# Two input projections of the second layer as seven block products each, instead of plain tiled matmuls

## The chip, the cores and the metric

The kernel runs on one core of one Trainium2 chip. The metric is the device time of one execution in microseconds (us). Three runs of the kernel before gave 672.19, 672.62 and 673.32 us; the median is 672.62 us.

## The reference, cut to what matters

The reference is a decoder trunk of two layers over 512 tokens with a width of 1024, all in float32. The first layer is an attention layer, the second a gated linear recurrence (HGRN2). Each layer ends with a normed residual and a gated embedding. What the change touches is the start of the second layer:

```python
u = rms_norm(h, norm_pre[1])            # (512, 1024)
proj = u @ w_in                         # (1024, 4096)
q, fl, inp, g = jnp.split(proj, 4, axis=-1)   # each (512, 1024)
...
y = (o * jax.nn.silu(gh))               # gh is g by heads; inp enters the recurrence as i
```

`inp` (called i below) and `g` are each a product of a 512x1024 matrix with a 1024x1024 matrix.

## The kernel before

Activations are kept transposed: `h[k]` is a tile of 128 features by 512 tokens, with k from 0 to 7. Every operand of a matmul is held as a pair of float32r tiles, high part and low part, and one product of float32 precision takes three matmuls (`three`, L138 to L142: high by high, low by high, high by low). Weights come from memory in tiles of 128x1024 (512 KB) into one of three slots `w_raw`; `load_w` and `split` (L272 to L274) then make the pair: ScalarE (ACT) writes `w_hi`, VectorE (DVE) writes `w_lo` as the difference. `w_hi` and `w_lo` have two slots each.

The end of the first layer is `layer_tail`. There `lin_c` makes four feature blocks of the gate at once and `lin_a` makes the blocks o = 4 to 7 one after the other, 24 matmuls each. Behind each block, `gated` (L387 to L391) updates `h[o]`, and `nxt` writes the pair `xg[o]` of `h[o]` times the gain (L281, L282) and adds the square of `h[o]` to `ss_acc` (L226, L230), from which the root mean square of the second layer's input is made.

Then i and g are made in four quarters q of 512 columns each by `lin_b_tok`: 4 weight tiles and 96 matmuls of 512 columns a quarter, with `xg` as the stationary and the weights as the moving operand. Quarters 0 and 1 are i (into tiles `it`, tag b3h), 2 and 3 are g (into `sg`, tag b3l). The factor per token `r1` is applied when ACT copies a bank out of PSUM (`evac_tok`, L733). `r1` comes from `st.rstd()`: four tiny products on TensorE (L236), one small DVE instruction (L239) and a power on GpSimd (L252); `spread` (L259, L263) makes it a full tile `rbc`. In the code `rstd` stands between quarter 0 and quarter 1, and `spread` behind the first weight tile of quarter 1. With `rbc`, DVE and ACT make the normed pair `u` (`scaled_norm`, L288 and `split`), which the recurrence uses. The first weight tile of the recurrence has a pair of its own, `w_f0`.

The order of the instructions on each engine is set at build time. A planner walks the program with estimated costs; on each engine it issues, of the instructions that are ready, the one that stands earliest in the program, unless `first()` lifts it. Inside `tc.manual_schedule(engines={PE})` the instructions of TensorE keep the order of the program. Each queue then runs strictly in its order. All weight loads are issued on SyncE's queue (SP).

Of the kernel before, what the change touches and what calls it, by code (L numbers as in the profile page):

```python
# [10 lines left out]
F32 = mybir.dt.float32  # L11
F32R = mybir.dt.float32r
# [8 lines left out]
P = 128  # L21
# [25 lines left out]
def tile_fox_hgrn2(  # L47
# [29 lines left out]
    def psB():  # L77
        return ps.tile([P, S], F32, name="psB", tag="B", bufs=6)
# [25 lines left out]
    def col(c):  # L104
        return vecs[:, c:c + 1]
# [11 lines left out]
    def load_w(ap, dst=None, raw=None, eng=ve):  # L117
        if raw is None:
            raw = fetch(ap)
        if dst is None:  # L120
            dst = (wp.tile([P, D], F32R, name="w_hi", tag="w_hi", bufs=2),
                   wp.tile([P, D], F32R, name="w_lo", tag="w_lo", bufs=2))
        hi, lo = dst
        if isinstance(hi, list):

            for i in range(2):
                split(hi[i], lo[i], raw[:, i * S:(i + 1) * S], eng)
        else:
            split(hi, lo, raw, eng)
        return hi, lo  # L130
# [57 lines left out]
    def lin_b_tok(chunks, src, half, ready=(), between=None, at=0):  # L188

        banks = [psA(), psA(), psB(), psB()] if half % 2 == 0 else [psB() for _ in range(4)]  # L190
        for kp in range(4):
            w = ready[kp] if kp < len(ready) else None
            if not isinstance(w, tuple):
                w = load_w(chunks[kp], raw=w)
            for j in range(2):
                k = 2 * kp + j
                f = slice(j * 512, (j + 1) * 512)
                for t in range(NT):
                    c = slice(t * P, (t + 1) * P)
# [55 lines left out]
    def spread(r, copy=True):  # L255

        rb = psB()
        for t in range(NT):
            pe.matmul(out=rb[:, t * P:(t + 1) * P], lhsT=r[:, t:t + 1].broadcast_to([P, P]), rhs=ident, start=True, stop=True)  # L259
        if not copy:  # L260
            return rb
        rs = tmp.tile([P, S], F32, name="rbc", tag="rbc", bufs=1)
        ac.copy(rs, rb)  # L263
        return rs

    def slots(tag, dt=F32R, ks=range(KT)):
        return [big.tile([P, S], dt, name=f"{tag}{k}", tag=f"{tag}{k}") for k in ks]
# [9 lines left out]
    def split_scaled(dst_hi, dst_lo, src, s):  # L277
        if isinstance(s, float):
            ins = ac.mul(dst_hi, src, s)
        else:  # L280
            ins = ac.activation(out=dst_hi, in_=src, func=AF.Copy, scale=s)  # L281
        ve.scalar_tensor_tensor(out=dst_lo, in0=src, scalar=s, in1=dst_hi.bitcast(F32), op0=ALU.mult, op1=ALU.subtract)  # L282
        return ins.ins

    def scaled_norm(dst, k, src, gcol, rb):

        un = t2("un")
        ve.scalar_tensor_tensor(out=un, in0=src, scalar=col(gcol + k), in1=rb, op0=ALU.mult, op1=ALU.mult)  # L288
        split(dst[0][k], dst[1][k], un)
# [46 lines left out]
            with first(o == KT - 1):  # L336
                ac.activation(out=self.zg[o], in_=b, func=AF.Copy, scale=col(C_NPOST[self.layer] + o))

    def layer_tail(layer, h, ah, zg, last=False):

        st = ah.st = Stat()
        ah.zg, hm = zg, ah.mem
        for g in ah.begun:
            for _ in g:
                pass
        for o in range(len(ah.begun), KT - 1):
            eng = gp if not last and o == len(ah.begun) else ve
# [16 lines left out]

        ws = [load_w(wgC[layer, c]) for c in range(2)]
        raws = [fetch(wgC[layer, c]) for c in range(2, 4)]

        def low(k):
            ve.tensor_tensor(out=hm[1][k], in0=h[k], in1=hm[0][k].bitcast(F32), op=ALU.subtract)

        with tc.manual_schedule(engines={DVE}):
            for k in range(KT):
                with first():
                    t = t2("zn")
                    ve.tensor_tensor(out=t, in0=rb, in1=zg[k], op=ALU.mult)
                    ve.tensor_tensor(out=h[k], in0=h[k], in1=t, op=ALU.add)
                    ac.copy(hm[0][k], h[k])
                    if k:
                        low(k - 1)
                if k in (4, 6):  # L380
                    ws.append(load_w(None, raw=raws[k // 2 - 2]))
            with first():
                low(KT - 1)
        for o, b in zip(LATE, eb):
            ac.copy(ah.ple(o), b)

        def gated(o, b, f=slice(0, S)):  # L387
            sg = t2("sgm")[:, f]
            ac.activation(out=sg, in_=b[:, f], func=AF.Sigmoid)  # L389
            ve.tensor_tensor(out=sg, in0=sg, in1=ah.ple(o)[:, f], op=ALU.mult)  # L390
            ve.tensor_tensor(out=h[o][:, f], in0=h[o][:, f], in1=sg, op=ALU.add)  # L391
            if last:
                nc.sync.dma_start(out[o][:, f], h[o][:, f])
            else:
                nxt(o)

        if not last:
            xg = pair_big("b2")
            stn = Stat()

            def nxt(o):
                split_scaled(xg[0][o], xg[1][o], h[o], col(C_NPRE[1] + o))
                stn.add(h[o])

        banks = lin_c(ws, hm)
        ws = [load_w(wgA[layer, o]) for o in range(2)]
        for o, b in enumerate(banks):
            gated(o, b)
        for o in range(4, KT):
            w = ws.pop(0)  # L410
            if last and o == KT - 1:
# [12 lines left out]
        return None if last else (xg, stn)
# [281 lines left out]
        nc.sync.dma_start(h[k], xT[:, k, :])  # L706
    att.close()
    turn[1] = 4
    xg, st = layer_tail(0, h, ah, slots("b3h", F32))

    l1 = ctx.enter_context(tc.tile_pool(name="l1", bufs=1))


    lmin = const.tile([P, 1], F32, name="lmin")
# [9 lines left out]
    it = slots("b3h", F32)  # L728
    sg = slots("b3l", F32)
    u = pair_big("b1")  # L730
    def evac_tok(q, banks):
        for t in range(NT):
            ac.activation(out=(it, sg)[q // 2][2 * t + q % 2], in_=banks[t], func=(AF.Copy, AF.Silu)[q // 2], scale=r1[:, t:t + 1])  # L733

    banks = lin_b_tok(wB1[0:4], xg, 0)
    r1 = st.rstd()
    rb = []
    banks1 = lin_b_tok(wB1[4:8], xg, 1, between=lambda: rb.append(spread(r1)))
    evac_tok(0, banks)
    for k in range(KT):  # L740
        scaled_norm(u, k, h[k], C_NPRE[1], rb[0])
    evac_tok(1, banks1)
    for q in range(2, 4):
        evac_tok(q, lin_b_tok(wB1[4 * q:4 * q + 4], xg, q))

    y = pair_big("b2")

# [1 line left out]
        pass  # L749


    w_f0 = load_w(wA1[8], [l1.tile([P, D], F32R, name=f"w_f0{q}") for q in range(2)])

    def general(rp):

# [299 lines left out]
    with tc.If(ok > 0) as cmp:  # L1055
        with tc.tile_pool(name="rec", bufs=2) as rp:
            ah = bounded(rp)
        layer_tail(1, h, ah, it, last=True)
    with cmp.Else():
        with tc.tile_pool(name="rec", bufs=2) as rp:  # L1060
            general(rp)
        ah = Ahead(1, y, ple_l1)
        ah.load(0)
        ah.room(u)
        ah.load1()
        for part in range(3):
            ah.load_emb(part)
        for o in EARLY:
            for _ in ah.early(o):
                pass  # L1070
        layer_tail(1, h, ah, it, last=True)


_INS = ["xT", "pT", "vec", "wfl", "wA0", "wB0", "wA1", "wB1", "wo", "wgC", "wgA", "wpl"]
# [61 lines left out]
```

## Time and profile before

| | |
|---|---|
| median of three runs | 672.62 us (672.19 to 673.32) |
| the profiled execution's own time | 672.09 us |
| its span in the profile | 670.3 us |
| TensorE busy in the span | 657.3 us, 98% |
| VectorE busy | 434.6 us, 65% |
| ScalarE busy | 336.9 us, 50% |
| GpSimd busy | 39.6 us, 6% |

The span runs from the first to the last instruction; the execution's own time is 1.8 us longer. TensorE's records overlap, since matmuls are pipelined, so its busy share is read as "had work", and its speed from the distance of starts. In the text, quarter 0 of i begins at 352.9 us of the span, and the recurrence's first matmul on `w_f0` at 441.9 us.

### The profile page before, as it was taken

Reading aid. Unit: us, or ns where it says so; the run is one execution under the profiler, and the core shown is the slowest. Engines: PE = TensorE matmul, PEld = TensorE weight load, DVE = VectorE, ACT = ScalarE, POOL = GpSimd, SP = SyncE. Lnnn points to the kernel's source line nnn. Section 1 sums busy time; section 2 is a strip of 40 time slices with the busy share of each in tenths; the row PEclk is TensorE's granted clock in tenths of the full one; section 3 lists DMA queues with packets and bytes.
Section 4 is the critical chain, followed back from the end, with each engine's and each line's share of the span. In section 5 each row is a group of like instructions: output and inputs, shape, how many; then the busy total and the mean of one; then the engine's idle time right before and its main releaser. Section 6 shows DMA issues by size and latency. Waiting matters only on the chain.

```text
span 670.3 us, 8922 instructions
## 1 busy us (share of the span) xinstructions
PE 657.3 (98%) x3226; PEld 548.4 (82%) x3226; DVE 434.6 (65%) x893; ACT 336.9 (50%) x656; POOL 39.6 (6%) x45
## 2 busy tenths in 40 slices
PE   8999999999999998999999999999999998999996
PEld 5888888888888877888888888888888887888886
DVE  7596223888888897337694372329888888233963
ACT  6457223766767685444563453344445455433431
POOL 1102200000000061001000110000010000001000
PEclk9999999999999999999999999999999999999999
DMA  7311326655555573221223223321122124122121
GB/s 283 130 64 65 128 95 189 165 151 133 153 139 139 150 230 100 95 95 37 92 92 125 84 79 109 135 68 64 63 70 89 63 93 135 56 96 95 58 107 59
DMA packets 26578, 73.22 MB, mean 109 GB/s; under 512 B 3808, under 2 KB 4192, under 8 KB 26528
## 3 DMA queue, kind: packets, MB, share of 16 engines
q1 hardware_dynamic: 26528, 72.59, 33.9%
q8 instruction: 27, 0.44, 0.3%
q14 instruction: 23, 0.19, 0.1%
HBM read 57.76 MB, written 2.10 MB: 89 GB/s over the span
## 4 chain that ended last, share of the span: by engine, by line
PE 92%; DVE 5%; ACT 1%; DMA 1%; issue 1%; POOL 0%; SPq 0%; ACTq 0%; DVEq 0%; POOLq 0%
PE psA L140 17%; PE psA L141 17%; PE psA L142 17%; PE psB L140 7%; PE psB L142 7%; PE psB L141 7%; PE psB L638 2%; PE psB L653 1%; PE psB L615 1%; PE psB L652 1%; PE psB L614 1%; PE psA L182 1%; PE psA L183 1%; PE psA L185 1%; PE psB L183 1%; PE psB L185 1%
## 5 line engine op out<-in xcount | busy, mean ns | idle before, releaser
L274 DVE TENSOR_TENSOR w_lo<-w_raw,w_hi 128x1024 fp32r<-128x1024 f32 x91 | 111.6, 1228 | 104.1 <-ACT w_hi L273 98.8
L140 PE MATMUL psA<-b1h,w_hi 128*128 128x512 f32 (+1 forms) x384 | 154.6, 403 | 0.0
L142 PE MATMUL psA<-b1l,w_hi 128*128 128x512 f32 (+1 forms) x384 | 148.5, 387 | 0.0
L141 PE MATMUL psA<-b1h,w_lo 128*128 128x512 f32 (+1 forms) x384 | 148.2, 386 | 0.2 <-DVE w_lo L274 0.2
L273 ACT CAST w_hi<-w_raw 128x1024 fp32r<-128x1024 f32 x92 | 96.2, 1047 | 62.4 <-PE psB L141 42.1
L142 PEld LDWEIGHTS psA<-b1l,w_hi 128*128 128x128 f32 x384 | 72.1, 188 | 15.1
L140 PEld LDWEIGHTS psA<-b1h,w_hi 128*128 128x128 f32 x384 | 72.3, 188 | 12.9 <-ACT sgm L389 0.7
L141 PEld LDWEIGHTS psA<-b1h,w_lo 128*128 128x128 f32 x384 | 72.5, 189 | 12.6 <-DVE w_lo L274 0.6
L140 PE MATMUL psB<-w_hi,b2h 128*128 128x512 f32 x144 | 56.3, 392 | 0.0
L142 PE MATMUL psB<-w_lo,b2h 128*128 128x512 f32 x144 | 56.1, 389 | 0.0
L141 PE MATMUL psB<-w_hi,b2l 128*128 128x512 f32 x144 | 56.1, 389 | 0.0
L621 ACT ACTIVATE pp<-pp,nm 128x128 f32<-128x128 f32 (+3 forms) x64 | 36.2, 565 | 23.0 <-DVE nm L619 22.2
L619 DVE CUSTOM_DVE_ANT_0 pp<-psB,cmask 128x128 f32<-128x128 f32 (+3 forms) x64 | 30.7, 480 | 14.5 <-PE psB L638 11.2
L230 DVE TENSOR_TENSOR ss_acc<-ss_acc,sq 128x512 f32<-128x512 f32 x26 | 17.9, 690 | 28.9 <-ACT sq L226 28.7
L140 PE MATMUL psA<-b2h,w_hi 128*128 128x512 f32 x80 | 31.8, 397 | 0.0
L142 PEld LDWEIGHTS psB<-w_lo,b2h 128*128 128x128 f32 x144 | 27.0, 188 | 5.7
L141 PEld LDWEIGHTS psB<-w_hi,b2l 128*128 128x128 f32 x144 | 27.1, 188 | 5.5
L140 PEld LDWEIGHTS psB<-w_hi,b2h 128*128 128x128 f32 x144 | 27.0, 188 | 5.5
L274 DVE TENSOR_TENSOR PTl<-psB,PTh 128x128 fp32r<-128x128 f32 (+3 forms) x64 | 30.8, 482 | 1.0 <-ACT PTh L273 0.8
L638 PE MATMUL psB<-ident,pp 128*128 128x128 f32 x160 | 28.4, 276 | 2.9 <-DVE pp L624 1.5
L142 PE MATMUL psA<-b2l,w_hi 128*128 128x512 f32 x80 | 31.2, 390 | 0.0
L141 PE MATMUL psA<-b2h,w_lo 128*128 128x512 f32 x80 | 31.2, 390 | 0.0
(228 smaller groups left out, 1217.5 us busy)
## 6 DMA issues: line engine op xcount, KB each, us to landing
w_raw<-in_wA_dram SPq DMA_DIRECT2D x40, 512.0 KB, 3.2
w_raw<-in_wB_dram SPq DMA_DIRECT2D x23, 512.0 KB, 3.3
w_raw<-in_wo_dram SPq DMA_DIRECT2D x16, 512.0 KB, 3.8
h<-in_xT_dram SPq DMA_DIRECT2D x16, 256.0 KB, 6.0
h<-kh SPq DMA_DIRECT2D x32, 128.0 KB, 2.3
w_raw<-in_wgC_dram SPq DMA_DIRECT2D x8, 512.0 KB, 3.2
w_raw<-in_wgA_dram SPq DMA_DIRECT2D x8, 512.0 KB, 3.3
h<-qh SPq DMA_DIRECT2D x16, 128.0 KB, 2.3
```

The source lines that it names most:

```text
L140: pe.matmul(out=out_ps, lhsT=sta[0], rhs=mov[0], start=start, stop=False)
L141: pe.matmul(out=out_ps, lhsT=sta[1], rhs=mov[0], start=False, stop=False)
L142: pe.matmul(out=out_ps, lhsT=sta[0], rhs=mov[1], start=False, stop=stop)
L182: pe.matmul(out=b, lhsT=hi[:, c], rhs=src[0][k], start=k == 0, stop=False)
L183: pe.matmul(out=b, lhsT=lo[:, c], rhs=src[0][k], start=False, stop=False)
L185: pe.matmul(out=b, lhsT=hi[:, c], rhs=src[1][k], start=False, stop=k == KT - 1)
L230: ve.tensor_tensor(out=self.acc, in0=self.acc, in1=sq, op=ALU.add)
L273: ins = ac.copy(dst_hi, src)
L274: eng.tensor_tensor(out=dst_lo, in0=src, in1=dst_hi.bitcast(F32), op=ALU.subtract)
L619: ve.tensor_tensor_reduce(out=pp[:, :W], in0=sc[:, :W], in1=cmask[:, S - W:S], op0=ALU.add, op1=ALU.min, scale=1.0, scalar=-NEG, accum_out=nm)
L621: ac.activation(out=pp[:, :W], in_=pp[:, :W], func=AF.Exp, bias=nm, scale=-1.0, accum_out=den)
L638: pe.transpose(out=tp[:, kt * P:(kt + 1) * P], in_=pp[:, kt * P:(kt + 1) * P], identity=ident)
```

## The change

The 512x1024 by 1024x1024 product is cut into two by two blocks: the activations by token halves (rows) and feature halves (columns), the weights by 512x512 blocks. Instead of eight block products, seven are made, of sums and differences of blocks, and the results are sums of these seven. Each block product (`product`) takes 24 matmuls of 512 columns, with two weight tiles, and uses two PSUM banks of tag B; i and g together take 14 products.

- The sums of activation blocks (`SM_D` to `SM_G`) are made in the tail of the first layer by `pair`, behind `nxt(o)` for o = 4 to 7: two multiplications on ACT, four subtractions or additions of 128x256 on DVE, and one `split` of 128x1024, into `a_sum`, a pool of its own. For o below 4, `xg` is made for the first 256 tokens alone.
- The sums of weight blocks are made in place. `t1` (two tiles, with `w_f0`'s slots) is loaded with B11 and split, and then B12 is added by an accumulating DMA that GpSimd's queue issues (`more`). `t2s` is `t1` plus B22, added on DVE; B12 is then accumulated onto the tile of B22, and B21 onto `t2s`. In each matrix six tiles are accumulated, six are loaded plainly and two are added on DVE.
- The order of the products is p1, p2, p3, p6, p7, p4, p5; p1 and p2 take plain blocks. For i, `rstd` and `spread` both stand between p1 and p2, on TensorE in that order.
- The results are collected in the tiles `it` and `sg`: ACT copies p1, DVE adds each further product out of PSUM in place, 14 additions of 128x512 a matrix, and ACT applies `r1` in place (with Silu for g).
- `scaled_norm` stands in the program between i and g.

```diff
             def nxt(o):
-                split_scaled(xg[0][o], xg[1][o], h[o], col(C_NPRE[1] + o))
+                f = slice(0, S // 2 if o < 4 else S)
+                split_scaled(xg[0][o][:, f], xg[1][o][:, f], h[o][:, f], col(C_NPRE[1] + o))
                 stn.add(h[o])
+                if o >= 4:
+                    pair(h, o - 4)
...
+    a_sum = [[sums.tile([P, 4, TH], F32R, name=f"as{q}{k}") for k in range(4)] for q in range(2)]
+    def tsum(q, c):
+        return (l1, sums)[q].tile([P, D], F32, name=f"tsum{q}{c}", tag=f"tsum{q}{c}")
+    def pair(h, k):
+        un = []
+        for b in (k, k + 4):
+            un.append(t2("un"))
+            ac.mul(un[-1], h[b], col(C_NPRE[1] + b))
+        a11, a21, a12, a22 = [x[:, i * TH:(i + 1) * TH] for x in un for i in range(2)]
+        sm = tsum(1, k % 2).rearrange("p (j t) -> p j t", t=TH)
+        ve.tensor_tensor(out=sm[:, SM_D, :], in0=a21, in1=a22, op=ALU.subtract)
+        ve.tensor_tensor(out=sm[:, SM_E, :], in0=sm[:, SM_D, :], in1=a11, op=ALU.subtract)
+        ve.tensor_tensor(out=sm[:, SM_F, :], in0=a11, in1=a21, op=ALU.subtract)
+        ve.tensor_tensor(out=sm[:, SM_G, :], in0=a12, in1=sm[:, SM_E, :], op=ALU.add)
+        split(a_sum[0][k], a_sum[1][k], sm)
...
+    def product(kind, ws):
+        banks = [psB(), psB()]
+        for k in range(4):
+            w, f = ws[k // 2], slice(k % 2 * S, (k % 2 + 1) * S)
+            hi, lo = operand(kind, k)
+            for t in range(2):
+                c = slice(t * P, (t + 1) * P)
+                three(banks[t], (hi[:, c], lo[:, c]), (w[0][:, f], w[1][:, f]), k == 0, k == 3)
+        return banks
+    def block(m, i, j, c):
+        return wB1[8 * m + 4 * j + 2 * i + c]
+    def more(dst, ap):
+        gp.dma_start(dst, ap, accum_op=ALU.add)
+        return dst
...
+        t1 = [tsum(0, c) for c in CH]
+        for c in CH:
+            nc.sync.dma_start(t1[c], block(m, 0, 0, c))
+        w = loads(t1)
+        for c in CH:
+            more(t1[c], block(m, 0, 1, c))
+        p1 = product((0, 0), w)
+        w = [load_w(block(m, 1, 0, c)) for c in CH]
+        if between:
+            between()
+        for t in CH:
+            ac.copy(C(1, 0, t), p1[t])
+        p2 = product((0, 1), w)
+        b22 = [fetch(block(m, 1, 1, c)) for c in CH]
+        w = loads(b22)
+        plus(0, 0, p2, (1, 0))
+        end(0, 0)
+        p3 = product(SM_G, w)
+        t2s = [tsum(1, c) for c in CH]
+        for c in CH:
+            ve.tensor_tensor(out=t2s[c], in0=t1[c], in1=b22[c], op=ALU.add)
+            more(b22[c], block(m, 0, 1, c))
+        w = loads(t2s)
+        p6 = product(SM_E, w)
+        for c in CH:
+            more(t2s[c], block(m, 1, 0, c))
+        w = loads(b22)
+        plus(1, 0, p6, (1, 0))
+        plus(0, 1, p3, (1, 0), ALU.subtract)
+        p7 = product(SM_F, w)
+        w = loads(t2s)
+        plus(1, 1, p7, (1, 0))
+        p4 = product((1, 1), w)
+        w = loads(t1)
+        plus(1, 0, p4, (1, 1))
+        end(1, 0)
+        p5 = product(SM_D, w)
+        for i in CH:
+            plus(i, 1, p5, (i, 1), (ALU.add, ALU.subtract)[i])
+            end(i, 1)
...
-    banks = lin_b_tok(wB1[0:4], xg, 0)
-    r1 = st.rstd()
...
-    for q in range(2, 4):
-        evac_tok(q, lin_b_tok(wB1[4 * q:4 * q + 4], xg, q))
+    def rstd1():
+        nonlocal r1
+        r1 = st.rstd()
+        rb.append(spread(r1))
+    with tc.manual_schedule(engines={PE}):
+        token_major(0, it, rstd1)
+        for k in range(KT):
+            scaled_norm(u, k, h[k], C_NPRE[1], rb[0])
+        token_major(1, sg)
+    att.close()
...
-    w_f0 = load_w(wA1[8], [l1.tile([P, D], F32R, name=f"w_f0{q}") for q in range(2)])
+    w_f0 = load_w(wA1[8], [l1.tile([P, D], F32R, name=f"w_f0{q}", tag=f"tsum0{q}") for q in range(2)])
```

## Rows read from the trace of the kernel before

**Rows 1.** The page, part 1: busy us (share of the span) and instructions.

```profile
PE 657.3 (98%) x3226; PEld 548.4 (82%) x3226; DVE 434.6 (65%) x893; ACT 336.9 (50%) x656; POOL 39.6 (6%) x45
```

**Rows 2.** Windows: stretch, length, then busy us by engine, clock, DMA share, GB/s.

```profile
331.10:357.60 26.50, 26.50 (x118) 21.79 (x118) 25.88 (x38) 18.05 (x28) 0.00 (x0) 1.00 0.24 83
...
352.89:441.90 89.01, 89.01 (x401) 73.80 (x400) 33.54 (x43) 34.29 (x44) 3.82 (x6) 1.00 0.29 101
```

**Rows 3.** Lines by form, TensorE, 352.80 to 441.92 us: busy, mean ns, idle.

```profile
L140 PE MATMUL psB<-w_hi,b2h 128*128 128x512 f32 x96 | 37.6, 391 | 0.0
...
L140 PE MATMUL psA<-w_hi,b2h 128*128 128x512 f32 x32 | 12.5, 391 | 0.0
```

**Rows 4.** Waits of TensorE, whole span: total us, times, longest; the longest first.

```profile
PE psA L140 <- ACT b2h L281: 1.6, 1, 1.6
```

**Rows 5.** Timeline of the statistic: start, duration, engine, line [idle before, releaser].

```profile
374.75 0.94 PE L236 MATMUL psB<-ones,ss_acc 128*128 128x1 f32 x8
375.55 0.49 PE L140 MATMUL psB<-w_hi,b2h 128*128 128x512 f32 x1
...
375.73 0.16 DVE L239 TENSOR_SCALAR ms<-psB 128x4 f32<-128x4 f32 x1 [4.14 <-PE psB L236]
...
375.97 1.93 POOL L252 TENSOR_TENSOR rs<-ms,mhalf 128x4 f32<-128x4 f32 x1 [71.13 <-DVE ms L239]
...
377.94 0.69 ACT L733 ACTIVATE b3h<-psA,rs 128x512 f32<-128x512 f32 x1 [2.17 <-POOL rs L252]
...
381.14 1.05 PE L259 MATMUL psB<-ident,rs 128*128 128x128 f32 x8
381.95 0.48 PE L140 MATMUL psB<-w_hi,b2h 128*128 128x512 f32 x1
```

**Rows 6.** Lines by form, VectorE, 331.1 to 357.6 us, the tail.

```profile
L274 DVE TENSOR_TENSOR w_lo<-w_raw,w_hi 128x1024 fp32r<-128x1024 f32 x5 | 6.1, 1219 | 0.0
L282 DVE SCALAR_TENSOR_TENSOR b2l<-h,vecs,b2h 128x512 fp32r<-128x512 f32 x8 | 6.0, 747 | 0.2 <-ACT b2h L281 0.2
```

**Rows 7.** Timeline of VectorE at the end of the tail.

```profile
354.45 0.69 DVE L391 TENSOR_TENSOR h<-h,sgm 128x512 f32<-128x512 f32 x1
355.06 1.22 DVE L274 TENSOR_TENSOR w_lo<-w_raw,w_hi 128x1024 fp32r<-128x1024 f32 x1
356.19 0.75 DVE L282 SCALAR_TENSOR_TENSOR b2l<-h,vecs,b2h 128x512 fp32r<-128x512 f32 x1
356.86 0.69 DVE L230 TENSOR_TENSOR ss_acc<-ss_acc,sq 128x512 f32<-128x512 f32 x1
```

**Rows 8.** Timeline of VectorE near the span's end: additions of 128x256.

```profile
665.71 0.43 DVE L390 TENSOR_TENSOR sgm<-sgm,b3l 128x256 f32<-128x256 f32 x1 [1.99 <-ACT sgm L389]
666.17 0.42 DVE L391 TENSOR_TENSOR h<-h,sgm 128x256 f32<-128x256 f32 x1
```

**Rows 9.** Timeline of one weight tile: its slot's release, both parts, the next tile.

```profile
363.84 1.05 ACT L273 CAST w_hi<-w_raw 128x1024 fp32r<-128x1024 f32 x1 [4.34 <-PE psB L141]
...
364.92 1.22 DVE L274 TENSOR_TENSOR w_lo<-w_raw,w_hi 128x1024 fp32r<-128x1024 f32 x1 [4.17 <-ACT w_hi L273]
...
363.86 0.39 PE L140 MATMUL psA<-w_hi,b2h 128*128 128x512 f32 x1
```

**Rows 10.** Timeline of VectorE: an addition out of PSUM and what follows.

```profile
306.39 0.69 DVE L375 TENSOR_TENSOR zn<-psB,b3h 128x512 f32<-128x512 f32 x1 [2.42 <-PE psB L259]
307.12 0.69 DVE L376 TENSOR_TENSOR h<-h,zn 128x512 f32<-128x512 f32 x1
```

**Rows 11.** Timeline of VectorE: the norms of `u` with a weight tile between.

```profile
387.12 2.07 DVE L288 SCALAR_TENSOR_TENSOR un<-h,vecs,rbc 128x512 f32<-128x512 f32 x3
389.11 1.22 DVE L274 TENSOR_TENSOR w_lo<-w_raw,w_hi 128x1024 fp32r<-128x1024 f32 x1
390.25 1.89 DVE L274 TENSOR_TENSOR b1l<-un,b1h 128x512 fp32r<-128x512 f32 x3
```

**Rows 12.** The page, part 6: DMA issues, KB each, median us to landing.

```profile
w_raw<-in_wB_dram SPq DMA_DIRECT2D x23, 512.0 KB, 3.3
```

More of the change, by code (lines that the diff above doesn't have):

```diff
@@ L337, in evac, with layer_tail @@
                 ac.activation(out=self.zg[o], in_=b, func=AF.Copy, scale=col(C_NPOST[self.layer] + o))
-    def layer_tail(layer, h, ah, zg, last=False):
+    def layer_tail(layer, h, ah, zg, pair=None):
+        last = pair is None
         st = ah.st = Stat()
@@ L708, in tile_fox_hgrn2 @@
     turn[1] = 4
-    xg, st = layer_tail(0, h, ah, slots("b3h", F32))
     l1 = ctx.enter_context(tc.tile_pool(name="l1", bufs=1))
+    sums = att.enter_context(tc.tile_pool(name="sums", bufs=1))
+    TH = S // 2
+    SM_D, SM_E, SM_F, SM_G = range(4)
+    a_sum = [[sums.tile([P, 4, TH], F32R, name=f"as{q}{k}") for k in range(4)] for q in range(2)]
[13 more added lines that the diff above has]
+        split(a_sum[0][k], a_sum[1][k], sm)
+    xg, st = layer_tail(0, h, ah, slots("b3h", F32), pair)
     lmin = const.tile([P, 1], F32, name="lmin")
@@ L730, in tile_fox_hgrn2, with operand @@
     u = pair_big("b1")
-    def evac_tok(q, banks):
-        for t in range(NT):
-            ac.activation(out=(it, sg)[q // 2][2 * t + q % 2], in_=banks[t], func=(AF.Copy, AF.Silu)[q // 2], scale=r1[:, t:t + 1])
-    banks = lin_b_tok(wB1[0:4], xg, 0)
-    r1 = st.rstd()
-    rb = []
[L738 to L742, printed above, removed]
-    for q in range(2, 4):
-        evac_tok(q, lin_b_tok(wB1[4 * q:4 * q + 4], xg, q))
+    def operand(kind, k):
+        if isinstance(kind, int):
+            return [a_sum[q][k][:, kind, :] for q in range(2)]
+        row, c = kind
+        return [xg[q][k + 4 * c][:, row * TH:(row + 1) * TH] for q in range(2)]
@@ new lines, in tile_fox_hgrn2, with token_major, C, plus @@
+    CH = range(2)
+    def token_major(m, dst, between=None):
+        def C(i, j, t):
+            return dst[2 * (2 * i + t) + j]
+        def plus(i, j, bank, src, op=ALU.add):
+            for t in CH:
+                ve.tensor_tensor(out=C(i, j, t), in0=bank[t], in1=C(*src, t), op=op)
+        def end(i, j):
+            for t in CH:
+                q = 2 * i + t
+                ac.activation(out=C(i, j, t), in_=C(i, j, t), func=AF.Silu if m else AF.Copy, scale=r1[:, q:q + 1])
+        def loads(raws):
+            return [load_w(None, raw=raw) for raw in raws]
+        t1 = [tsum(0, c) for c in CH]
[8 more added lines that the diff above has]
+            between()
+        for t in CH:
+            ac.copy(C(1, 0, t), p1[t])
[27 more added lines that the diff above has]
+            end(i, 1)
@@ L746, in tile_fox_hgrn2 @@
+    r1 = None
+    rb = []
+    def rstd1():
[8 more added lines that the diff above has]
+    att.close()
     y = pair_big("b2")
@@ L1057, in tile_fox_hgrn2 @@
             ah = bounded(rp)
-        layer_tail(1, h, ah, it, last=True)
+        layer_tail(1, h, ah, it)
     with cmp.Else():
@@ L1070, in tile_fox_hgrn2 @@
                 pass
-        layer_tail(1, h, ah, it, last=True)
+        layer_tail(1, h, ah, it)
 _INS = ["xT", "pT", "vec", "wfl", "wA0", "wB0", "wA1", "wB1", "wo", "wgC", "wgA", "wpl"]
```

## The prediction

> **What bounds the kernel now.** I read the page first. TensorE has work in 98% of the span, and no other engine comes near [rows 1]. A busy share alone could hide waits, so I looked at the list of TensorE's waits: the longest is 1.6 us, and it lies at the start of the kernel [rows 4]. Then I took the window that the change rebuilds, from the first matmul of i to the first of the recurrence: 89.01 us, TensorE busy throughout, its clock at 1.00 [rows 2], with 384 weight matmuls, 128 on each of three lines, of which the one is shown [rows 3]. The two breaks for the statistic cost 0.80 us (374.75 to 375.55) and 0.81 us (381.14 to 381.95) [rows 5]. So a matmul costs (89.01 - 1.61) / 384 = 0.2276 us, and 24 of them 5.46 us. This stage is bound by TensorE alone; VectorE works 33.5 of its 89 us [rows 2].
>
> The reader should look just as hard at the 26.5 us before and around its start. In the tail of the first layer VectorE is busy for 25.88 of 26.50 us [rows 2]. TensorE doesn't notice, because what VectorE finishes last, the sum of squares at 356.86 + 0.69 = 357.55 us [rows 7], isn't needed until 374.75 us [rows 5]. There are 17 us of cover there, and they are what the change spends.
>
> **The matmuls removed.** Fourteen products of 24 are 336 matmuls, 48 fewer: 48 x 0.2276 = -10.9 us. Shapes and operand types stay, so I take the same price.
>
> **The statistic, moved.** Now quarter 0 is followed by a mean, and the spread comes a weight tile later, so the way from the mean's end (375.55) over VectorE (375.73) and GpSimd (375.97 and 1.93 us) to the first reader (377.94) runs beside matmuls [rows 5]. After the change mean and spread follow each other on TensorE, with nothing between: 377.94 - 375.55 = 2.4 us in which TensorE stands still. This is sure, as its order is fixed. p2 and all behind it queue up there.
>
> And the mean comes after 24 matmuls, not after 96: if p1 starts at 352.9, it ends at 358.4, while the sum of squares was ready at 357.55 before any work was added to VectorE. What is added ahead of it: the planner takes the earliest ready instruction of the program, and `pair` for blocks 0 to 2 stands ahead of `gated(7)`. One `pair` is four operations of 128x256, 0.43 us each and 0.46 from start to start where one feeds the next [rows 8], and a low part of 128x1024, which takes 1.13 us of the queue (355.06 to 356.19) [rows 7]: 4 x 0.44 + 1.13 = 2.9 us, three of them 8.7 us. Half of `xg` for four blocks saves 4 x 0.26 = 1.0 us (0.69 for 128x512 less 0.43 for 128x256 [rows 8, 10]). The gaps that can be filled are 26.50 - 25.88 = 0.6 us. So the sum of squares ends at 357.55 + 8.7 - 1.0 - 0.6 = 364.6 us. Of the weight tiles' low parts in that window two belong to the new stage; if none of them gets ahead of it, it is 2.3 us earlier, 362.3; if the added work on ScalarE (per pair two multiplications and a cast, some 2.5 us) makes VectorE wait here and there, I allow 1 us more, 365.6. I take 364.6, as both weight tiles ran in that place before [rows 6, 7].
>
> Then p2 begins at 364.6 + 0.8 + 2.4 + 0.8 = 368.6. Without any wait it would begin at 352.9 + 5.5 + 1.6 = 360.0. Loss: +8.6 us (6.3 to 9.6). p1 itself may start up to six us late without changing this, since TensorE waits for the sum of squares anyway. p3 waits for the fourth pair (2.9 us) and four more weight tiles (4 x 1.13): 364.6 + 7.4 = 372.0, in time for 368.6 + 5.5 = 374.1. Loss there: nothing.
>
> **Weight tiles, twice as fast.** A tile now feeds 12 matmuls, not 24. Its successor's high part starts when its slot is free, at the start of the next tile (363.84 against 363.86), and the low part ends at 364.92 + 1.22 = 366.14, 2.30 us later [rows 9]. It is needed by the third matmul of the tile after: 2.73 + 0.46 = 3.19 us. Slack 0.9 us, where there were 3.6. An instruction on VectorE that starts just before it costs 0.6 (out of PSUM, 306.39 to 307.12 for one that feeds the next, 0.6 otherwise [rows 10]), 0.66 (norms, 387.12 to 389.11 for three [rows 11]) or 1.13 us (a weight sum). Most fit, two in a row don't.
>
> VectorE's sum for i, from p2's start to p5's end, six products or 32.8 us: 12 low parts at 1.13 (13.6), two weight sums (2.3), ten additions out of PSUM at 0.65 (6.5), the norms of `u` at (1.99 + 1.80) / 3 = 1.26 each (10.1; 1.80 is 1.89 less the overlap of 0.08 that the norms show, 2.07 against 1.99), and the fourth pair (2.9): 35.4 us. That is 2.6 us too much if the norms, which stand ahead of g in the program, all run there; if they spill into g there is room, as g needs 14 x 1.13 + 2.3 + 14 x 0.65 = 27.2 of 38.2 us. Between 0 and 2.6, I take 1.4. ScalarE has 14 casts of 1.05 us and 10 smaller pieces a matrix and stays well under 38 us.
>
> **The accumulating DMAs.** No row shows one. A plain load of 512 KB lands in 3.3 us [rows 12]. An accumulating one reads a second stream, so I bound it by 3.3 and 9.9 us. The tightest is B12 onto B22's first tile: issued when the weight sum is made, some 3.6 us into p3 (two additions out of PSUM, one low part, one sum), needed when p7's first high part may start, 2 x 5.46 - 2.73 = 8.2 us into p3, with the slack of 0.9: 5.5 us. At 3.3 it costs nothing, at 9.9 it costs 4.4 us in i, and in g less, where VectorE is free earlier. For a doubled transfer, 6.6 us, it is 1 us late. The reload of `t1` for g is about as tight (5.46 - 2.30 = 3.2 us against 3.3). I take 0.6 us for all of it, nearer to the plain row, since two other tiles are always in flight unhurried. On GpSimd's queue the accumulations onto `t1` stand ahead of the power of the statistic, but they wait only for p1's split, done before 364. The Trainium skill (DMA: Bandwidth & Descriptors, Anatomy of one DMA) gives 2.0 us plus bytes over 436 GB/s for a DMA issued by GpSimd, an estimate of 3.2 us here; by it the sum would be 0.6 us lower.
>
> What moves without a price: 16 evacuations on ScalarE become additions and scalings beside other products; SyncE's queue issues fewer loads; `w_f0` in `t1`'s slots can be split once p5's second tile is, a product ahead of its use; the recurrence's pool lies where the sums lay and must wait for p5, but its first tiles are wanted after 24 more matmuls.
>
> **Sum.** -10.9 + 8.6 + 1.4 + 0.6 = -0.3 us. Against the profiled execution's own 672.09 (span 670.3 and 1.8 around it) that is 671.8; the median of the runs lies 0.5 higher, so I predict 672.3 us, **no change**. What a measurement can tell from no change is 0.2%, 1.3 us.
>
> **The rivals.** *Faster:* the sum of squares at 362.3, no late tiles. -10.9 + 6.3 + 0.3 = -4.3, 668.3 us; it gains visibly as soon as the waits sum up to less than 9.6 us. For it speaks that the weight tiles of the new stage are last in the program's order; against it that VectorE had 0.6 us free. 0.32.
>
> *Slower, p1 starves:* the same order puts p1's first low part behind all pairs: 362.3 + 2.9 + 1.1 = 366.3. p1 starts at about 365.9, ends at 371.3, and p2 starts 4.0 later at 375.3, 15.3 late: +4.4 us, 676.7 (the norms then find free time). It decides from p1 starting after 359. Against it: VectorE took those tiles in the gaps while ScalarE made `xg`'s high part (355.06, between 354.45 and 356.19 [rows 7]). 0.14.
>
> *Slower, the accumulations are late:* at 9.9 us or more, 4.4 in i and 3 in g less the 0.6 counted: +6.5, 679 us. 0.10.
>
> *Slower, the clock:* the granted clock is 1.00 in every stretch that I read [rows 2], and no idle time is longer than 1.6 us [rows 4]; after the change TensorE stands idle from p1's end for up to 6 us. If the clock fell to its lower level (1.2 of 2.4 GHz) after that, half of p2 at double price would be 2.7 us: 675. The Trainium skill (TensorE: Matmul & The Clock Gate, Part 1) says that an idle engine's clock is halved until it has been busy again; no run here shows it. 0.10.
>
> **How the numbers follow.** The forecast has 0.34, for 671.3 to 673.9. Faster by over 0.2%: 0.32; slower: the three, 0.34. The range leaves out the best of the faster case and the late accumulations: 668.6 to 677.5 us.
>
> **What would show it.** In the profile after: 336 weight matmuls; TensorE idle between mean and spread for 2.4 us, released by GpSimd (right or wrong whatever the time); before the mean, a wait for `ss_acc` on VectorE, ending near 364.6; the first product's wait for `w_lo` short; later waits for `w_lo` under 3 us in all; the recurrence starting near 441.6. The forecast is wrong if the sum of squares ends before 362, if the clock drops below 1.00, or if waits name the accumulated tiles.

## The result, and the profile after

The changed kernel takes 680.64 us (median of 4 runs, 679.91 to 681.62) where the kernel before took 672.97 us in the runs beside it (median of 4): a ratio of 1.011, 95% interval 1.0094 to 1.0125. It is slower by 7.7 us. I had forecast no change (672.3 us, 668.6 to 677.5), so the forecast was wrong and the range did not hold the time.

The profiled execution took 681.62 us with a span of 679.9. This is its page, part 1 (it answers to [rows 1]), and part 2's line of the granted clock:

```profile
PE 657.7 (97%) x3178; PEld 545.5 (80%) x3178; DVE 480.0 (71%) x957; ACT 358.4 (53%) x684; POOL 49.8 (7%) x57
...
PEclk9999999999999999999996998999999999999999
```

The 48 matmuls are gone (3226 less 3178), yet TensorE is busy as long as before: 657.7 against 657.3 us. The matmuls that are left have become longer somewhere, and the clock line says where: two slices, both in the rebuilt stage, are below full speed. The stage itself now runs from 354.52 to 451.29 us, 96.77 us where it took 89.01 [rows 2]. That is +7.8 us, the whole result. (The stage also starts 1.6 us later than before; this arises in the first 11 us of the kernel, and the profiles of several changed kernels below do not have it.)

All waits of TensorE from 350 to 452 us, by the instruction that waits and what it waited for (total us, times, longest):

```profile
PE psB L142 <- DVE w_lo L274: 6.7, 3, 2.4
PE psB L259 <- POOL rs L252: 2.9, 1, 2.9
```

Before, TensorE was busy throughout this stage [rows 2]. Unstalled, the new stage would take 336 x 0.2276 + 1.61 = 78.1 us, so 18.7 us are lost, and these 9.6 us of waits are half of that. Much of the other half is in the windows of 5 us, read at their clock column (the third number from the end):

```profile
355.00:360.00 5.00, 2.83 (x10) 2.15 (x10) 5.00 (x9) 4.78 (x7) 1.05 (x1) 0.86 0.12 11
...
365.00:370.00 5.00, 3.83 (x15) 3.25 (x13) 5.00 (x10) 2.45 (x4) 0.47 (x2) 0.54 0.82 166
370.00:375.00 5.00, 3.22 (x12) 2.93 (x13) 2.46 (x3) 1.29 (x2) 1.73 (x1) 0.50 0.48 152
...
415.00:420.00 5.00, 3.18 (x8) 2.50 (x9) 2.90 (x3) 0.37 (x1) 0.00 (x0) 0.66 0.75 179
```

From 365 to 375 us TensorE has its lower level (1.2 of 2.4 GHz), and again near 417. Each time it had been waiting just before. The timeline of the first product and the statistic shows it, TensorE first, then VectorE and GpSimd:

```profile
354.76 0.39 PE L141 MATMUL psB<-w_hi,b2l 128*128 128x512 f32 x1
357.32 0.50 PE L142 MATMUL psB<-w_lo,b2h 128*128 128x512 f32 x1 [2.17 <-DVE w_lo L274]
...
363.91 0.51 PE L142 MATMUL psB<-w_lo,b2h 128*128 128x512 f32 x1 [2.12 <-DVE w_lo L274]
...
367.14 1.70 PE L236 MATMUL psB<-ones,ss_acc 128*128 128x1 f32 x8
371.78 2.08 PE L259 MATMUL psB<-ident,rs 128*128 128x128 f32 x8 [2.95 <-POOL rs L252]
373.51 0.77 PE L140 MATMUL psB<-w_hi,b2h 128*128 128x512 f32 x1
...
355.71 0.42 DVE L736 TENSOR_TENSOR tsum<-un 128x256 f32<-128x256 f32 x1
356.05 1.22 DVE L274 TENSOR_TENSOR w_lo<-tsum,w_hi 128x1024 fp32r<-128x1024 f32 x1
...
362.64 1.22 DVE L274 TENSOR_TENSOR w_lo<-tsum,w_hi 128x1024 fp32r<-128x1024 f32 x1
363.84 1.23 DVE L274 TENSOR_TENSOR as<-tsum,as 128x1024 fp32r<-128x1024 f32 x1
364.98 0.74 DVE L282 SCALAR_TENSOR_TENSOR b2l<-h,vecs,b2h 128x512 fp32r<-128x512 f32 x1
365.65 0.68 DVE L230 TENSOR_TENSOR ss_acc<-ss_acc,sq 128x512 f32<-128x512 f32 x1
...
369.55 0.15 DVE L239 TENSOR_SCALAR ms<-psB 128x4 f32<-128x4 f32 x1
...
369.79 1.94 POOL L252 TENSOR_TENSOR rs<-ms,mhalf 128x4 f32<-128x4 f32 x1 [4.53 <-DVE ms L239]
```

p1 starts at 354.52 and is stopped twice, because the low parts of its two weight tiles stand among the pairs' operations in VectorE's queue (356.05 and 362.64). Without a wait p1 takes 24 x 0.2276 = 5.46 us; it took 12.6. The sum of squares ends at 365.65 + 0.68 = 366.33. The mean starts 0.81 us after that, at 367.14, because p1 is not done earlier; the list above has no wait of TensorE for the sum. Then everything between p1 and p2 runs at the lower level: the mean's eight products take 1.70 us where they took 0.94 [rows 5], the spread takes 373.51 - 371.78 = 1.73 from its start to the next matmul's where it took 0.81, and 2.9 us lie idle between them. p2 starts 11.9 us later than p1's start, 5.46 us of matmuls and the two breaks of before would give.

The second loss is in g. ScalarE, VectorE and TensorE around g's p2:

```profile
411.87 1.04 ACT L273 CAST w_hi<-w_raw 128x1024 fp32r<-128x1024 f32 x1
...
414.41 1.22 DVE L826 TENSOR_TENSOR tsum<-tsum,w_raw 128x1024 f32<-128x1024 f32 x1 [3.03 <-DMA tsum<-in_wB_dram]
415.55 2.35 DVE L274 TENSOR_TENSOR w_lo<-w_raw,w_hi 128x1024 fp32r<-128x1024 f32 x2
...
416.82 0.79 PE L142 MATMUL psB<-w_lo,b2h 128*128 128x512 f32 x1 [2.38 <-DVE w_lo L274]
```

p2's first high part is ready at 412.91. Its low part needs nothing more, but stands in VectorE's queue behind a weight sum for p6, two products ahead, and that sum waits for an accumulating transfer. TensorE stands still, then runs slowly: g's p2 takes 9.6 us where 5.5 would do.

### The profile page after: what moved, and what is told of

The parts are those of the page before. It is cut to its first block, busy times and chain, and to the rows that moved or that the text cites. A ratio compares the mean times of both kernels' runs of the same rounds, so it can differ in the third digit from the quotient of the medians.

```text
span 679.9 us, 8979 instructions
## 1 busy us (share of the span) xinstructions
PE 657.7 (97%) x3178; PEld 545.5 (80%) x3178; DVE 480.0 (71%) x957; ACT 358.4 (53%) x684; POOL 49.8 (7%) x57
## 4 chain that ended last, share of the span: by engine, by line
PE 83%; DVE 9%; ACT 3%; issue 2%; DMA 2%; POOL 1%; SPq 0%; DVEq 0%; ACTq 0%; POOLq 0%
PE psA L140 15%; PE psA L141 15%; PE psA L142 15%; PE psB L140 6%; PE psB L142 6%; PE psB L141 6%; PE psB L644 2%; DVE w_lo L274 2%; DMA tsum<-in_wB_dram 1%; PE psB L659 1%; PE psB L621 1%; PE psB L658 1%; PE psB L620 1%; PE psA L182 1%; PE psA L183 1%
## 5 line engine op out<-in xcount | busy, mean ns | idle before, releaser
L140 PE MATMUL psA<-b1h,w_hi 128*128 128x512 f32 (+1 forms) x384 | 154.6, 403 | 0.0
L142 PE MATMUL psA<-b1l,w_hi 128*128 128x512 f32 (+1 forms) x384 | 148.6, 387 | 0.0
L141 PE MATMUL psA<-b1h,w_lo 128*128 128x512 f32 (+1 forms) x384 | 148.2, 386 | 0.1
L274 DVE TENSOR_TENSOR w_lo<-w_raw,w_hi 128x1024 fp32r<-128x1024 f32 x87 | 106.6, 1227 | 56.8 <-ACT w_hi L273 56.4
L273 ACT CAST w_hi<-w_raw 128x1024 fp32r<-128x1024 f32 x88 | 92.1, 1047 | 42.1 <-PE psB L141 21.7
L142 PEld LDWEIGHTS psA<-b1l,w_hi 128*128 128x128 f32 x384 | 72.1, 188 | 15.1
L140 PEld LDWEIGHTS psA<-b1h,w_hi 128*128 128x128 f32 x384 | 72.3, 188 | 12.9 <-ACT sgm L391 0.7
L141 PEld LDWEIGHTS psA<-b1h,w_lo 128*128 128x128 f32 x384 | 72.5, 189 | 12.6 <-DVE w_lo L274 0.6
L142 PE MATMUL psB<-w_lo,b2h 128*128 128x512 f32 x96 | 39.9, 416 | 6.8 <-DVE w_lo L274 6.7
L140 PE MATMUL psB<-w_hi,b2h 128*128 128x512 f32 x96 | 39.8, 417 | 0.0
L141 PE MATMUL psB<-w_hi,b2l 128*128 128x512 f32 x96 | 39.5, 412 | 0.0
L140 PE MATMUL psA<-b2h,w_hi 128*128 128x512 f32 x80 | 31.8, 397 | 0.0
L274 DVE TENSOR_TENSOR PTl<-psB,PTh 128x128 fp32r<-128x128 f32 (+3 forms) x64 | 30.8, 481 | 1.0 <-ACT PTh L273 0.8
L142 PE MATMUL psA<-b2l,w_hi 128*128 128x512 f32 x80 | 31.2, 391 | 0.0
L141 PE MATMUL psA<-b2h,w_lo 128*128 128x512 f32 x80 | 31.2, 389 | 0.0
L273 ACT CAST PTh<-psB 128x128 fp32r<-128x128 f32 (+3 forms) x64 | 26.9, 422 | 5.8 <-PE psB L644 4.9
L142 PEld LDWEIGHTS psB<-w_lo,b2h 128*128 128x128 f32 x96 | 19.2, 200 | 13.0 <-DVE w_lo L274 8.8
L630 DVE TENSOR_SCALAR pp<-pp,rden 128x128 f32<-128x128 f32 (+3 forms) x64 | 27.3, 426 | 1.0
```

What stands on the lines that cost most here:

```text
L140: pe.matmul(out=out_ps, lhsT=sta[0], rhs=mov[0], start=start, stop=False)
L141: pe.matmul(out=out_ps, lhsT=sta[1], rhs=mov[0], start=False, stop=False)
L142: pe.matmul(out=out_ps, lhsT=sta[0], rhs=mov[1], start=False, stop=stop)
L273: ins = ac.copy(dst_hi, src)
L274: eng.tensor_tensor(out=dst_lo, in0=src, in1=dst_hi.bitcast(F32), op=ALU.subtract)
L630: ve.tensor_scalar(out=pp[:, :W], in0=pp[:, :W], scalar1=rden, scalar2=None, op0=ALU.mult)
```

## The experiments

**The clock by itself.** Matmuls of zeros in bf16, whose result nothing reads, stand in TensorE's queue where it waited: 10 and 15 in i's p1, 12 between mean and spread, 11 in g's p2.

```
         r1 = st.rstd()
+        warm(12)            # 12 matmuls of a zero tile into a spare bank
         rb.append(spread(r1))
...
-        p1 = product((0, 0), w)
+        p1 = product((0, 0), w, (0, 0) if m else (10, 15))
```

> The changed kernel, with small bf16 matmuls on zeros into an unused bank put where TensorE stood idle: 10 and 15 of them inside p1 of i, 12 between mean and spread, 11 inside p2 of g. They compute nothing that is used. Theory A, idle time drops the clock and the half-speed matmuls are 6.8 us of the loss, but p1's late weight tiles and the sum of squares stay where they are: the clock stays at 1.00, and the time falls by 3 to 5 us, to about 676.5. Theory B, only VectorE's queue counts and the clock is a by-product: within 1 us of 680.6, with longer waits in the same places.

677.02 us, ratio 1.0054 (1.0037 to 1.0072). The stretch that had the clock at 0.50 now reads:

```profile
370.00:375.00 5.00, 3.84 (x21) 3.34 (x22) 4.51 (x6) 0.66 (x2) 1.10 (x1) 1.00 0.39 116
```

The clock stays at 1.00 in every window of the stage and 3.6 us come back, without any wait being cured. So about half of the 7.7 us by which the kernel became slower was TensorE's own speed after waits.

**The statistic later.** The mean stands behind p2 and the spread behind p3.

```
-        if between:
-            between()
         p2 = product((0, 1), w)
+        if between:
+            between[0]()        # mean
         p3 = product(SM_G, w)
+        if between:
+            between[1]()        # spread
```

> The changed kernel with the mean behind p2 and the spread behind p3, so that both have a product to cover them. Theory A, the place of the statistic costs the 2.9 us of the chain and the wait for the sum of squares: p3 starts 4 to 6 us earlier, about 675.5. Theory B, VectorE can't have the sums of x and six weight tiles ready sooner: p3 waits for them instead and starts at most 2 us earlier, 679 or more.

679.54 us, ratio 1.0091 (1.0074 to 1.0108). p3 of i started 5.3 us earlier against p1's start, as theory A had it (B: at most 2); the time is B's all the same, for g's p1, which had not waited before, waited 4.45 us for a low part and ran at the lower level behind it. The gain was given back 30 us later, which neither theory had.

**VectorE's work given to GpSimd.** In one kernel the four operations of each pair, in the other the sums of weight tiles.

```
-        ve.tensor_tensor(out=sm[:, SM_D, :], in0=a21, in1=a22, op=ALU.subtract)
+        gp.tensor_tensor(out=sm[:, SM_D, :], in0=a21, in1=a22, op=ALU.subtract)
...
-            ve.tensor_tensor(out=t2s[c], in0=t1[c], in1=b22[c], op=ALU.add)
+            gp.tensor_tensor(out=t2s[c], in0=t1[c], in1=b22[c], op=ALU.add)
```

> The changed kernel with the four additions and subtractions of each pair on GpSimd. Theory B, VectorE's queue sets p1's weight tiles and the sum of squares: some 1.6 us less in each of four pairs, p1's tiles and the mean come 4 to 6 us earlier, about 675. Theory A alone, without the queue: no more than the clock's share, 679. If GpSimd slows VectorE or is itself too slow for the fourth pair, p3 waits and the gain is lost.

> The changed kernel with the sum of t1 and B22 on GpSimd, not on VectorE. If the stall in p2 of g (2.5 us and some 1.6 us at the lower clock) comes from VectorE standing in its queue for the accumulating DMA, with finished casts behind it: the stall goes, 676.5. If the accumulated tile itself is late for its use, the stall moves to p6 of g and the time stays within 1.5 us of 680.6.

The pairs on GpSimd: 687.28 us, ratio 1.0198 (1.0171 to 1.0225), a clear miss. The power of the statistic stands behind the pairs in GpSimd's queue, and the spread waits 9.3 us for it. The weight sums on GpSimd: 679.33 us, ratio 1.0093 (1.0069 to 1.0118). g's p2 loses its stall (5.8 us in place of 9.6), and in the profile g gains 2.8 us, but i loses 2.0, so little arrives at the end. A row of GpSimd and one of VectorE in this run tell why a sum on GpSimd is not free:

```profile
364.12 2.81 POOL L826 TENSOR_TENSOR tsum<-tsum,w_raw 128x1024 f32<-128x1024 f32 x1
...
364.61 2.87 DVE L230 TENSOR_TENSOR ss_acc<-ss_acc,sq 128x512 f32<-128x512 f32 x1
```

The last sum of squares took 2.87 us in place of 0.68, and ended 0.55 us after GpSimd's sum; the mean then waited 0.86 us for it. The Trainium skill (SBUF — State Buffer, Who interferes with whom) says that an instruction of VectorE with two inputs in SBUF contends with a GpSimd instruction that reads SBUF, through a shared pair of ports that it calls an exclusive lock; the trace agrees.

**VectorE's order in i.** The pairs are traced behind the statistic instead of inside the tail; then also the spread behind p2; then also the weight sums on GpSimd.

```
                 stn.add(h[o])
-                if o >= 4:
-                    pair(h, o - 4)
...
         if between:
             between()
+            for k in range(4):
+                pair(h, k)
```

> The four pairs of block sums are traced behind the loads of p1 and p2 and behind the statistic, instead of inside the tail of layer one; VectorE then has one pair, not four, ahead of the last sum of squares. Theory B (VectorE's queue order): both waits of 2.2 us inside p1 of i go, the sum of squares ends before p1 does, p2 starts some 4.5 us behind p1's end (about 364.5 instead of 373.5), p3 may then wait 1 to 3 us for the last sums; the stall in g's p2 stays. In all about 674, between 672 and 677; clock at its upper level up to the end of p1. Theory A (idle TensorE alone): the same places gain, since the idle time that pulled the clock down is gone; A alone would give no more than the 3.6 us of the filled run, 677. Rival (VectorE over-full, work is only pushed back): p3 waits for the sums as long as p1 did, and time stays at 679 to 682.

> As e5, and the spread of the norm's reciprocal root stands behind p2 instead of ahead of it, the mean stays ahead of p2. Theory B: the 2.9 us between mean and spread are covered by p2; 2 to 3 us below e5, about 671.5. Rival (VectorE over-full): the norms of x, which wait for the spread, come later, and g's p1 waits for its weight tiles as it did when the whole statistic was moved (4.5 us there): no gain over e5, or a loss up to 2.

> As e6, and the four sums of weight tiles run on GpSimd, so that VectorE does not stand behind an accumulating DMA in g. Both theories: the stall of 4.1 us in g's p2 goes, as in the run that moved these sums alone; VectorE has 4.9 us less to do. If nothing else is late: 680.6 less 8 (tail and statistic), 2.5 (spread) and 3 (g), about 667 to 669, below the kernel before (673.4 on this chip's last runs). Rival (VectorE over-full, its work only moves the wait): 672 to 676.

679.44, 679.06 and 679.55 us; ratios 1.0089 (1.007 to 1.0108), 1.0082 (1.0065 to 1.01), 1.009 (1.0063 to 1.0118). Theory B missed all three. The rival written beside it, VectorE over-full, had the first two times (679 to 682, and no gain over that, with 4.45 us of waiting in g's p1), though in the first p3's wait was only 0.83 us, and it missed the third (672 to 676). What I had expected of i did happen: in the second, p2 starts 8.3 us after p1 and not 19.0, with a single wait of 1.44 us in p1. But g's p2 starts at 413.70, 413.56 and 414.39 us, in the kernel with the later statistic at 414.05, and in the changed kernel at 413.83: whatever the order, the same place (within 1.6 us when counted from p1's start). What these have in common shows in a window over i, VectorE's busy time being the third after the stretch's length (before; after; the second of these three; then that one's timeline of VectorE and TensorE at g's p1):

```profile
350.00:410.00 60.00, 60.00 (x274) 49.77 (x273) 28.63 (x36) 24.91 (x34) 3.82 (x6) 1.00 0.28 97
```

```profile
350.00:410.00 60.00, 52.77 (x215) 42.44 (x213) 54.12 (x75) 37.06 (x50) 8.16 (x8) 0.89 0.47 106
```

```profile
350.00:410.00 60.00, 51.02 (x212) 38.70 (x211) 54.71 (x78) 38.34 (x52) 8.23 (x9) 0.95 0.48 111
```

```profile
402.88 1.88 DVE L274 TENSOR_TENSOR b1l<-un,b1h 128x512 fp32r<-128x512 f32 x3
404.68 2.35 DVE L274 TENSOR_TENSOR w_lo<-tsum,w_hi 128x1024 fp32r<-128x1024 f32 x2
...
405.95 0.80 PE L142 MATMUL psB<-w_lo,b2h 128*128 128x512 f32 x1 [4.45 <-DVE w_lo L274]
```

VectorE has 54 us of work in these 60 where it had 28.6. Up to g's p1 it is full, and the norms of `u` (`un`, `b1l`), which nothing needs before the recurrence, stand ahead of g's first weight tiles. Moving work about inside i moved only the place of the wait. From here on the rival is theory C: VectorE is the engine that sets g's start.

**The load moved out of i, and the sum moved back in the queue.** Three kernels: the norms held behind g's first weight tiles, on top of the better order; the weight sums held behind p3's weight tiles, alone on the changed kernel; and both on top of the better order.

```
-        for k in range(KT):
-            scaled_norm(u, k, h[k], C_NPRE[1], rb[0])
         token_major(1, sg)
+        with tc.issue_after(held[0]):      # g's p1: its second low part
+            for k in range(KT):
+                scaled_norm(u, k, h[k], C_NPRE[1], rb[0])
...
+        with tc.issue_after(low[0]):       # p3's second low part
             for c in CH:
                 ve.tensor_tensor(out=t2s[c], in0=t1[c], in1=b22[c], op=ALU.add)
-                more(b22[c], block(m, 0, 1, c))
+        for c in CH:
+            more(b22[c], block(m, 0, 1, c))
```

> As e6, and the eight norms of x (11.4 us of VectorE) are held behind the weight tiles of g's p1 instead of standing in i. Theory C (VectorE is full from 350 to 408: 54.7 of 60 us in e6, and every earlier edit only moved the wait along its queue): the wait of 4.45 us in g's p1 and the lower clock behind it go, and part of the waits before p6 of i; g's p1 starts near 399 (400.9 in e6) and g's p2 near 405 (413.6 in e6); 8 us less than e6, about 671, between 668 and 675. Rival D (the accumulating transfers from GpSimd's queue set g's start): the accumulation is waited for just as before, g's p2 stays near 412, and time is 677 to 680.

> The changed kernel with one edit of order: the two sums of weight tiles, which wait for an accumulating transfer, are held behind the weight tiles of p3 in VectorE's queue. Theory of the queue's head: g's p2 loses its wait of 2.4 us and its lower clock (9.6 to 5.6 us), and as the sum is then made later, p6 may wait up to 1 us; 680.6 less 3 to 4, about 677. Theory C for i: nothing changes up to g's p1. Rival (the transfer itself is late for whoever needs it): g's p2 is free of the wait, and p6 of g waits 2 to 4 us in its place; time stays at 680.

> Both edits on top of e6: the norms of x behind g's p1, the sums of weight tiles behind p3's weight tiles. Theory C with the queue's head: i as in e8, g without a wait; at or a little below e8, 668 to 671, that is below the kernel before. Rival D: as e8, 677 to 680.

Norms moved: 674.04 us, ratio 1.0008 (0.9995 to 1.0021). Five of the eight us that C promised; g's p1 takes 5.7 us where it took 12.7, but g's p2 now waits 2.26 us for a low part, once more behind the sum that waits for the transfer. Rival D's place for g's p2, near 412, did not come: it starts at 407.65. Sums moved, alone: 679.9 us, ratio 1.0102 (1.0071 to 1.0133), not to be told from the changed kernel. g's p2 does fall from 9.6 to 5.4 us; p1, p7 and p4 of g each grow by 0.5 to 0.9, and in the profile g gains 2.1 us. That is less than the theory wanted, and the rival's long wait in p6 is not there either. Both: 671.62 us, ratio 0.9976 (0.9964 to 0.9988), faster than the kernel before by 0.24%, or 1.6 us; the interval lies below 1. Its window over i and TensorE's waits in the stage (the edit moves the lines of `split` by two: L275 and L276 are L273 and L274 above):

```profile
350.00:410.00 60.00, 55.92 (x242) 43.01 (x241) 51.60 (x71) 39.91 (x54) 8.22 (x9) 1.00 0.56 126
```

```profile
PE psB L142 <- DVE w_lo L276: 2.9, 4, 1.4
PE psB L140 <- ACT w_hi L275: 0.9, 1, 0.9
PE psB L141 <- DVE as L276: 0.8, 1, 0.8
PE psB L140 <- ACT as L275: 0.2, 1, 0.2
```

No wait is longer than 1.44 us and the clock is 1.00. The stage takes 441.95 - 354.21 = 87.74 us.

**Two checks on C.** The norms moved on the changed kernel alone; and on the best kernel, the additions of the pairs left out.

```
-        ve.tensor_tensor(out=sm[:, SM_D, :], in0=a21, in1=a22, op=ALU.subtract)
...
-        split(a_sum[0][k], a_sum[1][k], sm)
+        for i in range(2):
+            js = slice(2 * i, 2 * i + 2)
+            split(a_sum[0][k][:, js, :], a_sum[1][k][:, js, :], un[i].rearrange("p (j t) -> p j t", t=TH))
```

> The changed kernel with the eight norms held behind the weight tiles of g's p1, and nothing else: the pairs and the statistic stand where they stood. Theory C (VectorE is full up to g's p1, and in i the tail's pairs set p2's start): p2 of i starts as late as before this edit (372 to 374), so the 11.4 us taken off VectorE behind it free only g's p1 and part of g's p2; 677 to 680, though the same edit gave 5 us on top of the other order. Rival (the norms alone were the load that was too much, the order does not matter): as much as there, 675 to 676.

> The best order so far (norms behind g's p1, sums of weight tiles behind p3's), and the four additions of each pair of blocks of x left out: the operands of the products with sums are split from the scaled x itself, so the output is not the reference's. VectorE has 6.1 us less between 354 and 376. Theory C: the waits of 1.4, 0.8 and 0.9 us in i's p1, p3 and p6 go or halve, and time falls by 2 to 4 us, to 668 to 669.5. Rival (TensorE and the weights' transfers bound what is left): within 1 us of 671.6.

The norms alone: 681.52 us, ratio 1.0129 (1.0102 to 1.0155), above both ranges (677 to 680, 675 to 676); nothing gained, though VectorE's work from 350 to 410 falls to 44.8 us. p2 of i starts 19.2 us after p1, as late as in the changed kernel, and g's p2 waits 2.21 us as there. So load and order matter together: the order alone gave 1.6 us, the norms alone nothing, both 6.6 (680.64 less 674.04, each beside runs of before at 673). The additions left out: 670.6 us, ratio 0.9961 (0.995 to 0.9973), some 1 us below the best kernel, at the edge of the rival's range, and not the 2 to 4 expected. Even that 1 us is not clear: the intervals overlap, and in the profiles the stage is as long as in the best kernel (441.12 - 353.32 = 87.80 us against 87.74), only its start is 0.9 us earlier. TensorE's waits for VectorE fall only from 3.7 to 2.6 us, and p3 waits for ScalarE, whose list of casts and scalings is just as long there (40.0 us of the 60 from 350 to 410, 39.9 in the best kernel). First the window, then TensorE's timeline:

```profile
365.00:370.00 5.00, 3.35 (x18) 2.46 (x16) 3.58 (x6) 5.00 (x9) 0.00 (x0) 1.00 0.22 86
```

```profile
369.24 0.50 PE L140 MATMUL psB<-w_hi,as 128*128 128x512 f32 x1 [1.62 <-ACT w_hi L275]
```

ScalarE is busy for 5.00 of 5.00 us there, and behind the wait TensorE's clock fell (0.66 from 370 to 375 us). C holds up to the best kernel; beyond it VectorE is not the only limit in i.

## Why the prediction was wrong

Step by step, against the terms of the sum:

- *The matmuls removed*, -10.9: 48 fewer, right. The products whose operand is a sum of blocks cost more, though: 5.60 us each where those with blocks of x take 5.46, over eight products +1.1 us. "Shapes and operand types stay, so I take the same price" was 0.14 us a product too low.
- *When the sum of squares ends*, 364.6: right. It ended at 366.33, with the stage 1.6 us later than before, 364.7 when that is taken off. Three pairs stood ahead of it, as read from the planner's order; but no wait of TensorE ended with it (next point but one).
- *The chain from mean to spread*, 2.4 us of standing still: 2.9, right but for the clock.
- *The statistic, moved*, +8.6: it became 11.9 up to p2's start and 1.1 in p2, together 13.0. The step that failed is "p1 itself may start up to six us late without changing this, since TensorE waits for the sum of squares anyway". TensorE did not wait for the sum at all; of the signs I had named, the wait for `ss_acc` is missing, and p1's waits for `w_lo` were not short but 2.17 and 2.12 us. The low parts were late *inside* p1, not ahead of it, so p1 ended 0.8 us after the sum. And these waits lowered TensorE's clock: from 366.33 to p2's start 7.2 us went by in place of the 4.0 that I had added up at full speed, and p2 itself began at the lower level.
- *Rival, p1 starves* (676.7 us, 0.14): near the cause, in the wrong form. The pairs did hold up p1's low parts, but the first of them ran at 356.05, between pairs, and p1 started on time; it starved inside.
- *Rival, the clock* (675 us, 0.10): the right mechanism, at the wrong price and place. I priced half of p2, 2.7 us; the lower level also held the mean, the spread and a stretch in g. Filling the waits gave 3.6 us back. I had argued against it with a granted clock of 1.00 in stretches that held no long wait, which is no evidence about a kernel that has such waits. The Trainium skill (TensorE: Matmul & The Clock Gate, Part 1) was cited there for the halved clock of an idle engine; 0.50 from 370 to 375 us, after p1's waits, agrees with it. Not every wait of that length did this, though (last section).
- *Weight tiles, and accumulating DMAs*, +1.4 and +0.6: they became 0.44 in g's p1 and 4.13 in g's p2, 4.6 in all. The step that failed is "in g less, where VectorE is free earlier". I had asked whether a transfer is late for its own reader. It was late for the sum, which was in no hurry, and what stood *behind* the sum in VectorE's queue was. The transfers were inside my bounds: 5.5 us (median of 8 onto `tsum`) between 3.3 and 9.9. The Trainium skill's fit (DMA: Bandwidth & Descriptors, Anatomy of one DMA) gives an estimate of 3.2 us for a DMA from GpSimd of this size; these accumulating ones took 5.5, so here the measurement decides. The rival *the accumulations are late* (679 us, 0.10) came nearest to the measured time by luck: it wanted 9.9 us or more, and 4.4 us lost in i, where TensorE had no wait behind p2's start.

The sum with the measured sizes: -10.9 + 1.1 + 13.0 + 4.6 = +7.8 us, as found.

One more step was short, though in the changed kernel it did not show: I counted 35.4 us of VectorE's work for 32.8 us and took 1.4 us for it, since what spills into g would find room there. The runs with the better order show what a spill does: it lands ahead of g's first weight tiles and costs 4.45 us of waiting. Shown by runs: the clock's share, the sum's place together with the norms', and VectorE's load. Only read from the trace, and not tried by itself: what the queue's place of p1's two low parts costs with all else unchanged.

## What to carry to other kernels

When a change takes work from the engine that sets the time and gives other engines more, add up the busiest of these over the whole stretch, and ask of each of its instructions who waits for it and when; work that nobody needs yet must not stand ahead of work that somebody does. An instruction that waits for a slow transfer delays everything behind it in its queue, so what must be judged is the urgency of what follows it. A TensorE that is made to wait may come back at half its clock: count the work behind a wait at both prices, and don't take time "spent waiting anyway" as free.

## What the runs showed of the hardware that I had not expected

- The length of a wait did not tell whether TensorE's clock fell. In the changed kernel it fell behind waits of 2.1 to 2.4 us within products (matmuls then 0.43 us apart in place of 0.228), and in the best kernel, whose longest wait is 1.44 us, it stayed at 1.00. But with the norms moved, g's p2 waited 2.26 us and the clock stayed at 1.00 in both windows around it:

```profile
410.52 0.51 PE L142 MATMUL psB<-w_lo,b2h 128*128 128x512 f32 x1 [2.26 <-DVE w_lo L276]
```

```profile
405.00:410.00 5.00, 3.27 (x14) 2.17 (x12) 2.75 (x4) 4.03 (x6) 0.86 (x1) 1.00 0.92 161
410.00:415.00 5.00, 4.47 (x19) 3.68 (x20) 5.00 (x7) 2.29 (x3) 0.00 (x0) 1.00 0.65 202
```

  And in the first kernel of the order in i three waits of under 1 us each (0.83 us in p3, then these two in p6) were followed by 0.69:

```profile
377.34 0.50 PE L140 MATMUL psB<-w_hi,as 128*128 128x512 f32 x1 [0.69 <-ACT w_hi L273]
...
379.06 0.50 PE L142 MATMUL psB<-w_lo,as 128*128 128x512 f32 x1 [0.99 <-DVE w_lo L274]
```

```profile
380.00:385.00 5.00, 5.00 (x17) 3.91 (x16) 3.78 (x6) 2.71 (x4) 1.01 (x2) 0.69 1.05 208
```

  What decides it stays open here.
- The 24 matmuls of a product took 5.60 us when the stationary operand was one of the tiles `as`, 5.46 when it was a block of x, with the same moving tiles, shapes and types and at full clock. A mean matmul:

```profile
L142 PE MATMUL psB<-w_lo,as 128*128 128x512 f32 x64 | 25.3, 395 | 0.0
```

  In the kernel before, with blocks of x as the stationary operand, the three lines had 389 to 391 ns (391 is in [rows 3]). `w_f`, stationary too, already had 395 to 396 on all three lines there; other weight tiles as the stationary operand had, in their largest groups, 391 on L141 and L142, though 408 on L140. What sets these tiles apart stays open.
- A sum of 128x1024 on GpSimd stopped VectorE's next two-input operation until its end (2.87 us in place of 0.68), so two of them taken off VectorE's list left it with more busy time, not less: 57.3 of 60 us in the third kernel of the order in i, 54.7 in the second.
